# Low halves of weights: computed once, kept in DRAM and read back by later uses

## The chip, the cores and the metric

The kernel runs on one core of a Trainium2 chip. The metric is the device time of one execution in microseconds (us). Three timed runs of the kernel before gave 3698.6, 3701.6 and 3713.3 us, median 3701.6.

## What is computed

One inference step of a one-layer decoder trunk on 1024 prompt tokens and 8 sample tokens, all in float32. Cut to what matters here:

```
h  = rms_norm(x);  p = h @ w_in            # 7168 columns: q, k, v, conv inputs u, memory q, 3 gate blocks
a  = dilated attention(q, k, v);  m = attention into 256 memory tokens;  b = causal conv of the GLU of u
merged = gate_A * (a @ w_a_proj) + gate_B * (b @ w_b_proj) + gate_M * (m @ w_m_proj)
x1 = x + merged @ w_o
h2 = rms_norm(x1);  q = h2 @ w_pq          # 8 heads x 2 halves: product-key scores, top 16, experts and gates
y  = x1 + sum over chosen experts of gate * gelu(h2 . u_e) * v_e       # 16384 experts
```

## The kernel before, in words

**Split products.** A float32 matrix product is made of three matmuls (`mm3`, L173): each operand is split into a high half (a cast to a shorter format, in float32r) and a low half (what is left), and high x high, high x low and low x high are summed in PSUM. For weights this is done by `load_w` (L161). It takes one tile of 128x1024 float32 (512 KB) and three pools of buffers, two each: `wraw` for the loaded tile, `whi` for the high half, `wlo` for the low half. A DMA on SyncE's queue (SP) fills `wraw`, ScalarE (ACT) casts it into `whi` (L158), VectorE (DVE) subtracts the high half from it into `wlo` (L159). The names in the profile are `wr_`, `wh_` and `wl_` and the name of the weight.

**Stages.** `mem_stage` prepares the memory keys and values (8 weight tiles). `front(0)` does the first 512 prompt tokens and the 8 samples: projections k, v, q0, q1, q2, qm (24 weight tiles), conv inputs u (8), 24 gate tiles (`gate`, L652) and 12 tiles of the three branch projections (`gate_proj`, L671), with the attention between them. `tail("0")` does w_o (8 tiles) and, in `topk`, the 16 tiles of w_pq for these tokens. `front(1)` does the same 68 tiles for the second 512 prompt tokens. Then come two tails of 256 tokens each, `1a` and `1b`, again with 8 tiles of w_o (`o1a`, `o1b`) and 16 of w_pq (`pq1a`, `pq1b`) each. So the weights of the first half are loaded and split a second time for `front(1)`, and those of the tail a second and a third time. In tail 1a half of the w_pq tiles use a second set of buffers (`wx`, with one raw buffer). `peer_dense` (L1064) then runs through the 16384 experts densely for the first 640 tokens, while `peer_gather` (L957) fetches the chosen expert rows of the other 384 tokens and of the samples by indirect DMAs that GpSimd (POOL) issues, and DVE does their sums. `gate_build` (L1017) makes the dense gate matrix in DRAM (`gscr`, 2 MB a store) during `front(1)` and tail 1b.

**What sets the order.** The program is recorded with priorities, and a scheduler places each instruction by a model of the times. What results is a fixed order on each engine and on each engine's DMA queue. A DMA that waits for its buffer holds up every later DMA of its queue. TensorE (PE) takes its matmuls in the fixed order too.

## Time and profile before

| | |
|---|---|
| profiled execution, its own time | 3706.1 us |
| its span, first to last instruction | 3704.2 us |
| median of the three timed runs | 3701.6 us |
| TensorE matmul busy | 3434.1 us, 93% |
| TensorE weight load busy | 3014.3 us, 81% |
| VectorE busy | 2901.0 us, 78% |
| ScalarE busy | 1497.1 us, 40% |
| GpSimd busy | 577.5 us, 16% |
| DMA traffic | 902 MB, mean 244 GB/s |

The busy share of an engine over the whole span mixes stages. The stages can be told apart by the times at which ACT casts the tiles of each weight: `front(0)` and its tail take up to some 840 us, `front(1)` 840 to 1557 us, tail 1a 1557 to 1668 us, tail 1b 1658 to 1862 us, where the dense stage begins. A busy matmul row counts a matmul from its start to its modelled end, and these overlap; the weight load row does not overlap with itself.

### The profile page before, as it was taken

Reading aid. Unit: us, or ns where it says so; the run is one execution under the profiler, and the core shown is the slowest. Engines: PE = TensorE matmul, PEld = TensorE weight load, DVE = VectorE, ACT = ScalarE, POOL = GpSimd, SP = SyncE. Lnnn points to the kernel's source line nnn. Section 1 sums busy time; section 2 is a strip of 40 time slices with the busy share of each in tenths; the row PEclk is TensorE's granted clock in tenths of the full one; section 3 lists DMA queues with packets and bytes.
Section 4 is the critical chain, followed back from the end, with each engine's and each line's share of the span. In section 5 each row is a group of like instructions: output and inputs, shape, how many; then the busy total and the mean of one; then the engine's idle time right before and its main releaser. Section 6 shows DMA issues by size and latency. Waiting matters only on the chain.

```text
span 3704.2 us, 55195 instructions
## 1 busy us (share of the span) xinstructions
PE 3434.1 (93%) x19969; PEld 3014.3 (81%) x19969; DVE 2901.0 (78%) x6275; ACT 1497.1 (40%) x3517; POOL 577.5 (16%) x398
## 2 busy tenths in 40 slices
PE   8987989898899989887899999999989999999999
PEld 6766979697677778676798988989878889898988
DVE  4358555499998656779988888888878988897978
ACT  6554552235754445344443333333333333232322
POOL 0000000000000000000003333232323232332322
PEclk9997999999999989898799999999999999999999
DMA  5467455423354445763578988899889888888987
GB/s 182 132 207 256 149 199 157 150 90 116 109 185 168 167 168 188 253 214 131 196 237 315 341 318 326 304 351 327 323 296 350 317 333 324 317 331 299 341 301 273
DMA packets 338454, 902.09 MB, mean 244 GB/s; under 512 B 32588, under 2 KB 140276, under 8 KB 285436
## 3 DMA queue, kind: packets, MB, share of 16 engines
q1 hardware_dynamic: 281732, 487.49, 39.1%
q0 software_dynamic: 56448, 411.07, 28.9%
q8 instruction: 157, 2.57, 0.3%
q14 instruction: 117, 0.96, 0.1%
HBM read 804.09 MB, written 94.83 MB: 243 GB/s over the span
## 4 chain that ended last, share of the span: by engine, by line
PE 38%; issue 23%; DVE 15%; DMA 14%; POOL 8%; ACT 3%; SPq 0%; POOLq 0%; DVEq 0%; ACTq 0%
POOL uv L982 8%; DMA uv<-in_uv,idxB 4%; PE pg L175 2%; PE pg L174 2%; DMA vr<-in_v_tab 2%; PE pg L176 2%; PE pa L174 2%; PE pa L176 2%; PE pa L175 2%; PE pv L174 2%; PE pv L175 2%; PE pv L176 2%; PE pG L1058 1%; PE pG L1057 1%; DMA wko<-kscr 1%
## 5 line engine op out<-in xcount | busy, mean ns | idle before, releaser
L982 POOL DMA_INDIRECT uv<-in_uv,idxB x384 | 567.6, 1478 | 1529.0 <-DVE gacc L996 1196.1
L176 PE MATMUL pa<-h2Ah,ul 128*128 128x320 f32 x2048 | 633.9, 310 | 7.0 <-DVE ul L159 6.8
L174 PE MATMUL pa<-h2Ah,uh 128*128 128x320 f32 x2048 | 635.3, 310 | 2.6 <-ACT ge L1103 1.5
L175 PE MATMUL pa<-h2Al,uh 128*128 128x320 f32 x2048 | 634.0, 310 | 0.0
L986 DVE CUSTOM_DVE_ANT_0 uv<-uv,gh 128x1024 f32<-128x1024 f32 x392 | 477.1, 1219 | 122.1 <-DMA uv<-in_uv,idxB 117.8
L174 PE MATMUL pv<-vh,hh 128*128 128x512 f32 x1280 | 479.6, 396 | 41.5 <-ACT vh L158 28.4
L996 DVE SCALAR_TENSOR_TENSOR gacc<-uv,av,gacc 128x1024 f32<-128x1024 f32 x392 | 501.5, 1279 | 15.2 <-ACT av L994 9.5
L175 PE MATMUL pv<-vl,hh 128*128 128x512 f32 x1280 | 504.1, 394 | 5.2 <-DVE vl L159 5.0
L176 PE MATMUL pv<-vh,hl 128*128 128x512 f32 x1280 | 498.5, 393 | 0.0
L176 PEld LDWEIGHTS pa<-h2Ah,ul 128*128 128x128 f32 x2048 | 386.0, 189 | 11.9 <-DVE ul L159 8.6
L174 PEld LDWEIGHTS pa<-h2Ah,uh 128*128 128x128 f32 x2048 | 386.7, 189 | 7.4 <-ACT ge L1103 3.0
L175 PEld LDWEIGHTS pa<-h2Al,uh 128*128 128x128 f32 x2048 | 386.1, 189 | 2.4
L158 ACT CAST vh<-vr 128x512 fp32r<-128x512 f32 x256 | 157.5, 619 | 460.1 <-PE pv L176 239.4
L174 PEld LDWEIGHTS pv<-vh,hh 128*128 128x128 f32 x1280 | 242.5, 190 | 94.5 <-ACT vh L158 31.4
L175 PEld LDWEIGHTS pv<-vl,hh 128*128 128x128 f32 x1280 | 243.0, 190 | 56.8 <-DVE vl L159 8.8
L176 PEld LDWEIGHTS pv<-vh,hl 128*128 128x128 f32 x1280 | 242.8, 190 | 50.4
L982 POOL DMA_INDIRECT uv<-in_uv,idxS x8 | 9.2, 1156 | 1570.3 <-ACT co L740 1529.2
L159 DVE TENSOR_TENSOR vl<-vr,vh 128x512 fp32r<-128x512 f32 x256 | 175.2, 686 | 83.6 <-ACT vh L158 83.2
L174 PE MATMUL pg<-hTh,wh_g 128*128 128x260 f32 (+1 forms) x576 | 195.1, 339 | 4.0 <-ACT tg L660 4.0
L158 ACT CAST uh<-ur 128x1024 fp32r<-128x1024 f32 x128 | 134.2, 1048 | 152.5 <-PE pa L175 116.5
L175 PE MATMUL pg<-hTl,wh_g 128*128 128x260 f32 (+1 forms) x576 | 194.9, 338 | 0.0
L176 PE MATMUL pg<-hTh,wl_g 128*128 128x260 f32 (+1 forms) x576 | 194.4, 337 | 0.0
(558 smaller groups left out, 7524.1 us busy)
## 6 DMA issues: line engine op xcount, KB each, us to landing
ur<-in_uT SPq DMA_DIRECT2D x128, 512.0 KB
vr<-in_v_tab SPq DMA_DIRECT2D x256, 256.0 KB
gscr<-stg SPq DMA_DIRECT2D x20, 2048.0 KB
Gt<-gscr SPq DMA_DIRECT2D x32, 1280.0 KB
wr_g<-in_w_col SPq DMA_DIRECT2D x48, 512.0 KB
wr_q<-in_w_in SPq DMA_DIRECT2D x24, 512.0 KB
wr_u<-in_w_col SPq DMA_DIRECT2D x16, 512.0 KB
wr_pq<-in_w_col SPq DMA_DIRECT2D x16, 512.0 KB
```

Source lines behind the costliest of these rows:

```text
L158: nc.scalar.copy(hi, raw)
L159: nc.vector.tensor_tensor(lo, raw, hi.bitcast(F32), op=OP.subtract)
L174: nc.tensor.matmul(out, ah, bh, start=start, stop=False)
L175: nc.tensor.matmul(out, ah, bl, start=False, stop=False)
L176: nc.tensor.matmul(out, al, bh, start=False, stop=stop)
L982: nc.gpsimd.indirect_dma_start(out=uv, out_offset=None, in_=I["uv"], in_offset=bass.IndirectOffsetOnAxis(ap=col, axis=0),)
L986: nc.vector.tensor_tensor_reduce(out=uv[:, 0:D], in0=uv[:, 0:D], in1=h2, scale=1.0, scalar=0.0, op0=OP.mult, op1=OP.add, accum_out=av[:, s ...
L996: nc.vector.scalar_tensor_tensor(acc, uv[:, D:], av[:, j : j + 1], acc, op0=OP.mult, op1=OP.add)
L1057: nc.tensor.matmul(pG[:, q], o2[:, a, :, q], wh[:, a, :, q], start=True, stop=False)
L1058: nc.tensor.matmul(pG[:, q], o2[:, a, :, q], wl[:, a, :, q], start=False, stop=True)
```

## The change

`load_w` gets a key. At the first use of a key the tile is split as before, and the low half is also stored to a DRAM tile of its own by a DMA that GpSimd issues. At a later use of the same key ACT casts the high half as before, and the low half is loaded from that DRAM tile by a second DMA on SP's queue, in place of the subtraction on DVE. The keys do not hold the number of the half or of the tail, so `front(1)` and the tails 1a and 1b read what `front(0)` and tail 0 stored. The memory stage and the dense stage have no keys.

```diff
+        lows = {}
+
-        def load_w(wp, src, a, b, name, nraw=2):
+        def load_w(wp, src, a, b, name, nraw=2, key=None):
+
             raw = wp.tile([P, 1024], F32, tag="wraw", bufs=nraw, name=f"wr_{name}")
             hi = wp.tile([P, 1024], F32R, tag="whi", bufs=2, name=f"wh_{name}")
             lo = wp.tile([P, 1024], F32R, tag="wlo", bufs=2, name=f"wl_{name}")
             nc.sync.dma_start(raw.rearrange("p (a b) -> p a b", a=a), src)
-            split_load(raw, hi, lo)
+            if key in lows:
+                nc.scalar.copy(hi, raw)
+                nc.sync.dma_start(lo.bitcast(F32), lows[key])
+            else:
+                split_load(raw, hi, lo)
+                if key is not None:
+                    lows[key] = dram.tile([P, 1024], F32, name=f"low_{key}")
+                    nc.gpsimd.dma_start(lows[key], lo.bitcast(F32))
...
-                        wh, wl = load_w(wp, w_in[:, 2 * kk : 2 * kk + 2, w0 : w0 + 512], 2, 512, f"{name}{hf}{kk}")
+                        wh, wl = load_w(wp, w_in[:, 2 * kk : 2 * kk + 2, w0 : w0 + 512], 2, 512, f"{name}{hf}{kk}", key=f"{name}_{kk}")
...
-                    gh, gl = load_w(wp, w_col[8 + gi], KD, P, f"g{hf}{gi}")
+                    gh, gl = load_w(wp, w_col[8 + gi], KD, P, f"g{hf}{gi}", key=f"g_{gi}")
...
-                wh, wl = load_w(wx if own else wp, w_col[32 + hc], KD, P, f"pq{tid}{hc}", 1 if own else 2)
+                wh, wl = load_w(wx if own else wp, w_col[32 + hc], KD, P, f"pq{tid}{hc}", 1 if own else 2, key=f"pq_{hc}")
```

The calls for u, the branch projections and w_o get a key in the same way. Counted over the program, 92 tiles are stored (24 + 8 + 24 + 12 in `front(0)`, 8 + 16 in tail 0) and 116 are loaded back (68 in `front(1)`, 24 in each of the tails 1a and 1b). The scheduler places everything anew, and line numbers move by 10 in the changed kernel.

At two places the order shows what moves. The first is SP's DMA queue in tail 1b, before: `wr_pq1b` are the raw tiles of w_pq, in the order of their numbers, `h2scr` is the store of the normed tokens.

```order
L165 DMA wr_pq1b_18274<-in_w_col 128x1024
L798 DMA x1scr<-x_1b_17967 128x1024
L798 DMA x1scr<-x_1b_17969 128x1024
L165 DMA wr_pq1b_18324<-in_w_col 128x1024
L801 DMA h2scr<-h_1b_18126 128x1024
L801 DMA h2scr<-h_1b_18149 128x1024
L165 DMA wr_pq1b_18374<-in_w_col 128x1024
L165 DMA wr_pq1b_18424<-in_w_col 128x1024
```

The same queue at the same place, in the changed kernel; `wl_pq1b_18460` is the low half of the tile whose raw load is `wr_pq1b_18458`, `low_pq` its copy in DRAM.

```order
L168 DMA wr_pq1b_18508<-in_w_col 128x1024
L808 DMA x1scr<-x_1b_18151 128x1024
L808 DMA x1scr<-x_1b_18153 128x1024
L811 DMA h2scr<-h_1b_18310 128x1024
L811 DMA h2scr<-h_1b_18333 128x1024
L171 DMA wl_pq1b_18460<-low_pq_7825 128x1024
L168 DMA wr_pq1b_18558<-in_w_col 128x1024
L171 DMA wl_pq1b_18510<-low_pq_7926 128x1024
L168 DMA wr_pq1b_18608<-in_w_col 128x1024
```

A low load now stands between the raw loads, ahead of the raw load of the tile two further on (18558 behind 18460), so that this raw load comes after the moment at which the low buffer is free.

The second place is DVE in the projections of `front(1)`, before: `oh`, `rk` and `iv` belong to the top-16 search of tail 0, `raw_q`, `ra_q` and `rb_q` to the rotary step of q.

```order
L214 TENSOR_TENSOR rb_q_0_12398<-raw_q_0_12381,c_rope 128x4x16
L217 TENSOR_TENSOR rb_q_0_12398<-raw_q_0_12381,c_rope 128x4x16
L205 TENSOR_TENSOR raw_q_128_12404<-raw_q_128_12404,c_qn_a 128x512
L908 TENSOR_TENSOR oh_9534<-oh_9534,iv_9453 128x2048
L159 TENSOR_TENSOR wl_q_12539<-wr_q_12537,wh_q_12538 128x1024
L220 TENSOR_TENSOR raw_q_0_12381<-ra_q_0_12397,rb_q_0_12398 128x4x32
```

The same step of q on DVE in the changed kernel.

```order
L224 TENSOR_TENSOR rb_q_0_12582<-raw_q_0_12565,c_rope 128x4x16
L227 TENSOR_TENSOR rb_q_0_12582<-raw_q_0_12565,c_rope 128x4x16
L922 TENSOR_TENSOR oh_9718<-oh_9718 128x128x8
L868 CAST iv_9737<-ix_7818 128x256
L215 TENSOR_TENSOR raw_q_128_12588<-raw_q_128_12588,c_qn_a 128x512
L230 TENSOR_TENSOR raw_q_0_12565<-ra_q_0_12581,rb_q_0_12582 128x4x32
```

The subtraction between the search and the rotary step is gone; of 216 subtractions for weight tiles on DVE 100 are left.

## Rows read from the trace of the kernel before

**Rows 1.** The page's part 1: busy time, share, instructions.

```profile
PE 3434.1 (93%) x19969; PEld 3014.3 (81%) x19969; DVE 2901.0 (78%) x6275; ACT 1497.1 (40%) x3517; POOL 577.5 (16%) x398
```

**Rows 2.** Stretches: length; busy PE, PEld, DVE, ACT, POOL (instructions); clock, DMA share, GB/s.

```profile
204.00:351.00 147.00, 112.11 (x657) 94.52 (x655) 106.01 (x492) 65.56 (x210) 0.00 (x0) 0.84 0.76 254
...
842.00:1016.00 174.00, 150.22 (x655) 118.03 (x655) 171.63 (x721) 114.36 (x298) 0.00 (x0) 0.96 0.35 109
...
1557.00:1600.00 43.00, 31.34 (x110) 22.74 (x109) 33.09 (x42) 13.17 (x22) 5.01 (x4) 0.88 0.75 282
1600.00:1668.00 68.00, 59.13 (x446) 56.78 (x444) 53.32 (x209) 32.22 (x56) 0.00 (x0) 0.92 0.55 188
1668.00:1698.00 30.00, 25.38 (x119) 19.76 (x118) 29.94 (x152) 10.16 (x15) 0.00 (x0) 1.00 0.45 156
1698.00:1795.00 97.00, 76.40 (x559) 71.55 (x560) 96.97 (x331) 49.79 (x81) 4.00 (x2) 0.89 0.40 147
...
1862.00:3704.00 1842.00, 1784.60 (x9889) 1617.51 (x9887) 1567.07 (x2110) 598.29 (x1343) 561.48 (x380) 0.99 0.86 316
```

**Rows 3.** Waits of PE in 200:420, 800:1000, 1200:1400, 1700:1870: us in total, times, longest.

```profile
PE pS_w L319 <- DVE wao L321: 19.8, 14, 6.1
...
PE p_q L175 <- DVE wl_q L159: 10.3, 4, 6.1
...
PE wT L380 <- DMA wkp<-kscr: 10.2, 3, 7.6
PE wT L380 <- DMA wko<-kscr: 7.2, 3, 3.0
...
PE tr_t1b L190 <- DVE h_1b L183: 11.2, 1, 11.2
```

**Rows 4.** Groups of instructions: busy us, mean ns of one, then idle before them.

```profile
L159 DVE TENSOR_TENSOR wl_g<-wr_g,wh_g 128x1024 fp32r<-128x1024 f32 x48 | 58.7, 1222 | 58.5 <-ACT wh_g L158 58.3
...
L174 PEld LDWEIGHTS pq1b<-h2h1b,wh_pq1b 128*128 128x128 f32 x128 | 25.9, 204 | 7.5 <-ACT wh_pq1b L158 6.4 <-ACT h2h1b L170 1.1
```

**Rows 5.** Stretches, of line L159 (subtractions) alone: length, DVE busy, clock, DMA.

```profile
842.00:1016.00 174.00, 28.84 (x24) 0.96 0.35 109
1016.00:1557.00 541.00, 53.71 (x44) 0.93 0.53 185
1557.00:1862.00 305.00, 62.17 (x51) 0.87 0.53 191
```

**Rows 6.** Timeline of ACT by tile: casts, ns min/median/max, first and last start.

```profile
L158 ACT CAST wh_k<-wr_k x4: 1047/1047/1051, 841.9 to 870.4; 128x1024 fp32r<-128x1024 f32 x4
...
L158 ACT CAST wh_u<-wr_u x8: 1031/1047/1059, 1016.4 to 1091.7; 128x1024 fp32r<-128x1024 f32 x8
...
L158 ACT CAST wh_pq1b<-wr_pq1b x16: 1038/1047/1062, 1697.9 to 1790.2; 128x1024 fp32r<-128x1024 f32 x16
```

**Rows 7.** Timeline of PE in the dense stage, 512-column matmuls: start, us.

```profile
3698.17 0.39 PE L175 MATMUL pv<-vl,hh 128*128 128x512 f32 x1
...
3699.76 0.39 PE L176 MATMUL pv<-vh,hl 128*128 128x512 f32 x1
```

**Rows 8.** Timeline of SP's queue, DMA issues: start, us of the issue.

```profile
1647.42 0.38 SPq L165 DMA_DIRECT2D wr_o1b<-in_w_o  x1
```

**Rows 9.** The chain of work that ended last, 1215:1345 and 1580:1870: start, us.

```profile
1233.36 11.45 DMA wko<-kscr
...
1302.08 15.60 DMA wko<-kscr
...
1610.76 5.14 DMA h2scr<-h_1a
1615.98 3.98 DMA wr_pq1a<-in_w_col
...
1662.90 4.48 DMA wr_pq1a<-in_w_col
...
1739.91 3.28 DMA wr_pq1b<-in_w_col
```

More of the change, by code (lines that the diff above doesn't have):

```diff
@@ L564, in front @@
                     glu = mx.tile([P, 30 + NT], F32, tag="glu", bufs=2, name=f"glu{hf}{cb}")
-                    u1h, u1l = load_w(wp, w_col[cb], KD, P, f"u1{hf}{cb}")
-                    u2h, u2l = load_w(wp, w_col[4 + cb], KD, P, f"u2{hf}{cb}")
+                    u1h, u1l = load_w(wp, w_col[cb], KD, P, f"u1{hf}{cb}", key=f"u1_{cb}")
+                    u2h, u2l = load_w(wp, w_col[4 + cb], KD, P, f"u2{hf}{cb}", key=f"u2_{cb}")
                     for c0, cn in chunks:
@@ L672, in gate_proj @@
                     for fp in range(4):
-                        ph, pl = load_w(wp, w_pr[br][:, :, fp * 256 : fp * 256 + 256], 4, 256, f"p{br}{hf}{fp}")
+                        ph, pl = load_w(wp, w_pr[br][:, :, fp * 256 : fp * 256 + 256], 4, 256, f"p{br}{hf}{fp}", key=f"p{br}_{fp}")
                         for f in (2 * fp, 2 * fp + 1):
@@ L779, in tail @@
                         for kk in range(4):
-                            wh, wl = load_w(wp, w_o[:, 2 * kk : 2 * kk + 2, gs], 2, 512, f"o{tid}{cg}{kk}")
+                            wh, wl = load_w(wp, w_o[:, 2 * kk : 2 * kk + 2, gs], 2, 512, f"o{tid}{cg}{kk}", key=f"o{cg}_{kk}")
                             for j in range(2):
```

## The prediction, made before the changed kernel ran

> **What bounds the kernel now.** I read the page's busy times first: PE 93%, DVE 78% [rows 1]. That average hides where DVE is the limit, so I cut the span into stages and read busy time by stretch [rows 2]. The dense stage, 1862 to 3704 us, is half of the time: PE 1784.6 of 1842 us, DVE 1567.1. It has no keyed weights, so nothing of the change reaches it but its start; I keep its length. In two stretches ahead of it DVE is full. **Stretch A** is the projections of `front(1)`, 842 to 1016 us: DVE 171.6 of 174 us, while the weight loads of PE fill only 118.0. **Stretch B** is the tails: DVE 29.9 of 30 us in 1668 to 1698 and 97.0 of 97 us in 1698 to 1795, with PE's weight loads at 19.8 and 71.6. The waits of PE say the same: 10.3 us for low halves of q, 11.2 us for the normed rows of 1b, both from DVE [rows 3]. In 1600 to 1668 us (the w_pq tiles of 1a) PE's weight loads take 56.8 of 68 us and DVE 53.3: there PE is the limit, and DVE's relief is worth little.
>
> **What is removed.** 116 subtractions, one 1.22 us [rows 4]. In stretch A they are 24, 28.8 us; in the rest of `front(1)` 44, 53.7 us; in the tails 51 subtractions stand in 1557 to 1862 us with 62.2 us [rows 5], of which some 47 are keyed, 57 us. Only what lies where DVE is the limit is gained.
>
> *Stretch A.* 24 tiles go from 841.9 to 1016.4 us, 7.27 us a tile [rows 6]. DVE without the subtractions needs 171.6 - 28.8 = 142.8 us: 31 us less than the stretch. PE needs 24 matmuls of 512 columns a tile; in an unhindered row they start 1.59 / 7 = 0.227 us apart [rows 7], so 5.45 us a tile, 131 us: 43 us less. So DVE stays the nearer limit, with at most 31 us to gain. An engine at 98.6% owes that to a backlog that can always be worked on; once its reserve is gone it will wait for PE now and then. I take 0.7 of it: **-22 us**, bounds -31 and 0.
>
> *Stretch B.* In 1698 to 1795 us stand the 16 subtractions of 1b, 16 x 1.22 = 19.5 us; 0.7 of it is 14 us. The 16 tiles of w_o and the wait of 11.2 us for the normed rows [rows 3] hang on DVE in part; I take 8 us for them together. **-22 us**, bounds -45 (all 57 us less what 1a cannot use, since PE is full there) and 0.
>
> **What is added to the second half.** 116 loads of 512 KB on SP's queue. The new chain for tile i: its low buffer is free when PE has finished tile i-2; then SP issues the load (0.38 us an issue [rows 8], 0.4 here), it lands L later, and PE may go on. Before, ACT and DVE filled that place in 1.05 + 1.22 us [rows 4, 6]. With two buffers a tile cannot take less than (L + 0.4 + p) / 2, p being PE's own time for a tile. The order on SP shows the low load ahead of the raw load of tile i+2, so it does not queue behind that one. L has no row, as no such load exists. The nearest are raw loads of the same size for which the chain waited: 3.28, 3.98 and 4.48 us [rows 9]; at the other end stand attention loads of half the size that came behind other transfers, 11.45 and 15.60 us [rows 9]. I take **L = 4.7 us**, near the first, because in A the DMA engines are busy at 0.35 and in 1b at 0.40 [rows 2], and add a little for the doubled traffic. The limits are then:
>
> - A, p = 5.45: (4.7 + 0.4 + 5.45) / 2 = 5.3 us, below the 5.95 us that DVE's 142.8 us allow.
> - pq1b, p = 24 x 0.204 = 4.9 [rows 4]: 5.0 us, against (1790.2 - 1697.9) / 15 = 6.15 us a tile now [rows 6].
> - o1a and o1b, p = 12 x 0.227 = 2.7: 3.9 us, against some 5.3 now (8 tiles in the 43 us of 1557 to 1600 us).
> - pq1a has two sets of buffers, four low halves in flight, and is not held by L.
>
> The Trainium skill, page "DMA: Bandwidth & Descriptors", section "Anatomy of one DMA", fits a DMA issued from GpSimd as 2.0 us plus its bytes at 436 GB/s, which for 512 KB makes an estimate of 3.2 us. The shortest of the three rows, 3.28 us, agrees and the other two are up to 1.3 us longer; with 3.2 us the w_o tiles would take 3.15 us, 16 x 0.75 = 12 us less, and the sum would be 3662 instead of 3674.
>
> In `front(1)` behind A a tile comes every (1557 - 1016) / 44 = 12.3 us, between attention work, so an L of up to some 11.8 us is hidden. Yet a low load that waits for PE holds up the attention loads behind it in the queue, and PE waits for such loads already, 10.2 + 7.2 us in 1200 to 1400 us [rows 3]. Against that DVE loses 53.7 us of work it has time for. I take **+6 us**, bounds -10 and +20. The traffic: B carries 305 x 191 GB/s = 58 MB [rows 5], plus 47 x 0.524 = 25 MB; in 283 us that is 293 GB/s. The dense stage shows 316 GB/s held for 1842 us [rows 2], so it fits, without much room.
>
> **What is added to the first half.** 92 stores of 512 KB from GpSimd's queue, which is empty there. A low buffer may be rewritten only when its store has landed. The tile two further on needs it: the low half of i is ready about when PE starts i-1 and its buffer's next content is needed at PE's start of i+2, three tiles of 30 x 0.227 = 6.8 us (30 matmuls with the samples' block), less 3.5 us for split and issue, so some 17 us of cover. The nearest row, a 512 KB store to DRAM, took 5.14 us [rows 9]. So the hold costs nothing; were the cover gone, each us beyond 17 would cost a us a tile. What remains is traffic: 48 MB. Only in 204 to 351 us are the DMA engines busy at 0.76 (254 GB/s) [rows 2], and PE waits there for attention on DVE, 19.8 us [rows 3], which waits for loads. The 8 stores of u fall into it, 4.2 MB, 16 us at that rate. I take **+6 us**, bounds 0 and +16.
>
> **Sum.** -22 - 22 + 6 + 6 = -32 us: 3706.1 - 32 = 3674 us against the profiled execution's own time. The median of the runs lies 4.5 us below that execution, so I forecast **3670 us**.
>
> **Rivals.**
>
> *The lows come late: slower.* Same chain, L = 9 us, as low loads queue behind 2 MB stores of `gscr`, `h2scr` stores and each other; the attention loads at 11 to 16 us [rows 9] speak for it, DMA shares of 0.35 to 0.45 against it. Then A takes 7.4 us a tile (+3 us), pq1b 7.1 (+15), w_o 6.05 (+12), with the +6 and +6 of above: +42, or 3744 as a median. It decides from L of about 7.5 us: there A gains 14 us, pq1b loses 4, w_o nothing, and with the +12 the sum is about zero.
>
> *Relief without gain.* DVE is freed, but PE then waits for low loads or for ACT about as long as it did for DVE (L of 6.5 to 8), or the scheduler's new order gives the gain back in the dense stage, where 57 us of idle PE time stand [rows 2] and shift with every order. For it: PE is 93% busy [rows 1]. Time 3690 to 3715, middle 3702.
>
> *More than forecast.* DVE's limit falls fully in A (-31) and B (-40), and the added waits stay at +6: -65, 3637 us.
>
> That the subtractions stay is no rival: the order has 100 of 216 left.
>
> **How the numbers follow.** Forecast (3650 to 3690) 0.45, relief without gain 0.24, late lows (3720 to 3790) 0.22, more than forecast 0.09. The range 3637 to 3745 leaves out about half of each outer case, 0.15. The forecast's own range is 3650 to 3690. Half a per cent, about what a measurement of this kernel can tell, is 18.5 us: faster below 3683, slower above 3720. Of the forecast 0.05 lies above 3683. So faster 0.40 + 0.09 = 0.49, same 0.24 + 0.05 = 0.29, slower 0.22.
>
> **What would show it.** A right: the 24 tiles of the projections in some 152 us instead of 174.5, with no PE wait for `wl_q`. B right: the 16 casts of pq1b in some 78 us instead of 92, the dense stage starting some 30 us earlier and lasting as long as before. L right: PE waits for `wl_` loads of a few us in all in the tails. Late lows would show as PE waits on DMA `wl_pq1b` and `wl_o1b` of over 30 us; a wrong first half as a later start of tail 0; a wrong dense stage as a length other than 1842 us by over 10 us.

## The result and the profile after

The changed kernel takes 3743.6 us in the median against 3700.9 us for the kernel before in the same comparison: ratio 1.0096, 95% interval 1.0073 to 1.0119 (the two medians alone give 1.0115). The time lies within the range given, but on the wrong side: it is slower, where faster was the likeliest. The profiled execution has a span of 3746.6 us, 42.4 more than before.

The page's part 1 of the changed kernel, to be held against [rows 1]: DVE has lost 116 instructions and 124 us, PE's work is the same, and the time went up all the same.

```profile
PE 3429.9 (92%) x19969; PEld 3016.1 (81%) x19969; DVE 2777.1 (74%) x6159; ACT 1499.8 (40%) x3516; POOL 616.0 (16%) x490
```

To find where, the times at which ACT casts the first tile of each weight are taken from both traces as marks [rows 6]. Here are three of them in the timeline of ACT of the changed kernel.

```profile
L170 ACT CAST wh_k<-wr_k x4: 1046/1048/1054, 870.7 to 901.2; 128x1024 fp32r<-128x1024 f32 x4
...
L170 ACT CAST wh_u<-wr_u x8: 1040/1051/1060, 1028.5 to 1100.5; 128x1024 fp32r<-128x1024 f32 x8
...
L170 ACT CAST wh_pq1b<-wr_pq1b x16: 1046/1050/1060, 1731.5 to 1820.1; 128x1024 fp32r<-128x1024 f32 x16
```

`front(1)` begins at 870.7 us instead of 841.9: **the first half lost 29 us**. The projections of `front(1)` (stretch A) take 157.8 us instead of 174.5: 17 gained. From there to o1a 546.7 instead of 540.7: 6 lost. From o1a to the last cast of pq1b 244.9 instead of 233.1: 12 lost. From there to the end 1926.5 instead of 1914.0: 12 lost. Together +42.

The stretches of the changed kernel, with the columns of [rows 2]: the branch projections of `front(0)` and w_o of tail 0, then stretch A, the w_pq tiles of 1b, and the dense stage.

```profile
579.00:674.00 95.00, 81.78 (x681) 76.00 (x681) 45.83 (x92) 20.81 (x29) 6.40 (x12) 0.98 0.66 205
674.00:740.00 66.00, 57.59 (x267) 43.27 (x267) 20.86 (x31) 11.05 (x13) 4.26 (x8) 0.95 0.58 185
...
870.00:1028.00 158.00, 147.31 (x664) 117.87 (x663) 152.19 (x727) 116.60 (x305) 0.00 (x0) 0.98 0.64 210
1731.00:1830.00 99.00, 82.90 (x615) 77.53 (x614) 87.26 (x320) 51.36 (x86) 4.57 (x4) 0.91 0.74 271
1890.00:3746.00 1856.00, 1786.79 (x9883) 1620.09 (x9881) 1558.99 (x2049) 595.41 (x1339) 550.80 (x380) 0.98 0.86 313
```

The first two lines are the loss of the first half: the same 12 and 8 tiles took 75.7 and 58.2 us before. PE now fills 81.78 of 95.00 us of the first; in the kernel before it filled nearly all of it:

```profile
577.00:653.00 76.00, 74.77 (x618) 73.64 (x617) 47.98 (x95) 21.06 (x30) 0.00 (x0) 1.00 0.54 165
653.00:711.00 58.00, 54.62 (x254) 40.53 (x254) 19.50 (x28) 10.16 (x12) 0.00 (x0) 1.00 0.40 132
```

Not all that the first stretch grew by is waiting. Between its marks it grew by 19.6 us: PE is idle for 12.0 us more, and busy for 7.6 us more. Its instructions rose from 618 to 681 because the new order places 72 of the 192 matmuls of the samples' attention (`spaw`) in it; before, all of them stood ahead of it.

What DVE waited for there, in the changed kernel from 579 to 740 us (us in total, times, longest):

```profile
DVE th L694 <- DMA th<-gtscr: 20.4, 8, 4.5
DVE merged L694 <- DMA th<-gtscr: 15.0, 6, 4.5
```

The same two waits in the kernel before, from 577 to 711 us:

```profile
DVE th L684 <- DMA th<-gtscr: 11.3, 8, 2.8
...
DVE merged L684 <- DMA th<-gtscr: 1.6, 1, 1.6
```

`th` are the gate tiles, 130 KB each, which each step of a branch projection reloads from `gtscr`; they have three buffers. 35 us of waits stand where 13 stood, and PE waits for DVE in its turn (`py` is its output for the branch projections, `po` for w_o). In the changed kernel, 579 to 674 us and then 674 to 740 us:

```profile
PE py L184 <- DVE th L694: 9.9, 7, 2.8
PE py L184 <- DVE merged L694: 3.1, 3, 1.6
...
PE po L184 <- DVE th L694: 6.7, 1, 6.7
```

In the kernel before, 577 to 653 us and then 653 to 711 us:

```profile
PE py L174 <- DVE th L684: 1.1, 4, 0.5
...
PE po L174 <- DVE th L684: 2.4, 1, 2.4
```

The landing of each reload can be counted from the traces, from the start of its issue on SP to its last landing record. Over the 48 reloads the median is 2.7 us in the kernel before (longest 4.0) and 4.3 us in the changed kernel (longest 6.6).

PE's waits for low halves in the second half, in 870 to 1028, 1575 to 1632, 1698 to 1731 and 1731 to 1830 us. They are there, some 22 us in all:

```profile
PE p_q L185 <- DMA wl_q<-low_q: 4.6, 3, 2.1
...
PE po1a L185 <- DMA wl_o1a<-low_o: 6.7, 4, 3.6
...
PE po1b L185 <- DMA wl_o1b<-low_o: 3.7, 4, 1.6
...
PE pq1b L186 <- DMA wl_pq1b<-low_pq: 6.6, 5, 3.5
```

How long a low load takes stands in the chain that ended last, tails of the changed kernel (start, us):

```profile
1645.96 5.02 DMA wl_pq1a<-low_pq
...
1709.69 4.57 DMA wl_o1b<-low_o
...
1754.43 6.41 DMA wl_pq1b<-low_pq
1763.82 4.59 DMA wl_pq1b<-low_pq
1782.24 7.20 DMA wl_pq1b<-low_pq
...
1803.52 11.93 DMA wl_pq1b<-low_pq
```

### The profile page after: what moved, and what is told of

Read it like the earlier page. It is cut to its first block, busy times and chain, and to the rows that moved or that the text cites. A ratio compares the mean times of both kernels' runs of the same rounds, so it can differ in the third digit from the quotient of the medians.

```text
span 3746.6 us, 55402 instructions
## 1 busy us (share of the span) xinstructions
PE 3429.9 (92%) x19969; PEld 3016.1 (81%) x19969; DVE 2777.1 (74%) x6159; ACT 1499.8 (40%) x3516; POOL 616.0 (16%) x490
## 4 chain that ended last, share of the span: by engine, by line
PE 22%; issue 20%; DMA 8%; POOL 6%; DVE 2%; ACT 1%; POOLq 0%; SPq 0%; DVEq 0%; ACTq 0%
POOL uv L992 6%; PE pa L184 3%; PE pa L185 3%; PE pa L186 3%; DMA uv<-in_uv,idxB 3%; PE pv L184 3%; PE pv L186 3%; PE pv L185 3%; DMA vr<-in_v_tab 2%; DMA wl_pq1b<-low_pq 1%; DMA uv<-in_uv,idxS 1%; DMA ur<-in_uT 1%; DVE gacc L1006 0%; DMA wl_o1b<-low_o 0%; PE pq1a L184 0%
## 5 line engine op out<-in xcount | busy, mean ns | idle before, releaser
L992 POOL DMA_INDIRECT uv<-in_uv,idxB x384 | 555.4, 1446 | 1534.8 <-DVE gacc L1006 1222.2
L184 PEld LDWEIGHTS pa<-h2Ah,uh 128*128 128x128 f32 x2048 | 386.6, 189 | 16.5 <-ACT ge L1113 9.3
L159 DVE TENSOR_TENSOR vl<-vr,vh 128x512 fp32r<-128x512 f32 x256 | 175.8, 689 | 96.0 <-ACT vh L158 95.7
L159 DVE TENSOR_TENSOR ul<-ur,uh 128x1024 fp32r<-128x1024 f32 x128 | 156.6, 1223 | 52.0 <-ACT uh L158 51.7
```

What stands on the lines that cost most here:

```text
L159: nc.vector.tensor_tensor(lo, raw, hi.bitcast(F32), op=OP.subtract)
L184: nc.tensor.matmul(out, ah, bh, start=start, stop=False)
L992: nc.gpsimd.indirect_dma_start(out=uv, out_offset=None, in_=I["uv"], in_offset=bass.IndirectOffsetOnAxis(ap=col, axis=0),)
```

## The experiments

All runs by the same marks, from one profiled execution each, in us: p is the length of the branch projections of `front(0)` (first cast of p to first cast of o), then the start of `front(1)`, stretch A, `front(1)` from its start to o1a, from o1a to the last cast of pq1b, and from there to the end. The ratio is that of the timed runs to those of the kernel before in the same comparison. A profiled execution need not be a typical one: that of `th4` was the slowest of ten, 18 us above their median, and that of `stores_only` the fastest of four, 20 us below it.

| kernel | p | front(1) starts | A | front(1) | tails | to the end | ratio (95%) |
|---|---|---|---|---|---|---|---|
| before | 75.7 | 841.9 | 174.5 | 715.2 | 233.1 | 1914.0 | 1 |
| before_again | 76.9 | 840.2 | 174.6 | 713.2 | 235.7 | 1900.5 | |
| after | 95.3 | 870.7 | 157.8 | 704.5 | 244.9 | 1926.5 | 1.0096 (1.0073-1.0119) |
| after_again | 97.8 | 869.2 | 157.1 | 702.7 | 244.4 | 1927.1 | |
| stores_only | 96.4 | 867.2 | 163.3 | 719.0 | 225.5 | 1926.5 | 1.0167 (1.0125-1.0208) |
| stores_quarter | 79.9 | 843.6 | 176.6 | 720.5 | 225.9 | 1957.6 | 1.0134 (1.0086-1.0181) |
| stores_tiny | 76.3 | 835.2 | 173.7 | 699.6 | 225.4 | 1934.3 | 1.0006 (0.9987-1.0025) |
| stores_halves | 89.7 | 854.4 | 155.3 | 685.5 | 241.8 | 1927.4 | 1.0059 (1.0038-1.0081) |
| loads_only | 77.0 | 842.3 | 162.7 | 692.8 | 235.2 | 1917.3 | 0.9991 (0.9963-1.0019) |
| no_lows | 76.9 | 838.5 | 161.0 | 682.4 | 214.7 | 1916.7 | 0.9865 (0.9828-0.9902) |
| keys_proj_u | 76.3 | 845.0 | 166.8 | 695.9 | 225.3 | 1939.7 | 1.0034 (1.0015-1.0053) |
| keys_front | 82.3 | 848.2 | 163.0 | 688.7 | 229.8 | 1945.9 | 1.0031 (1.0010-1.0052) |
| keys_no_p | 81.6 | 852.1 | 156.8 | 696.8 | 248.0 | 1897.9 | 0.9994 (0.9977-1.0011) |
| keys_no_po | 82.1 | 846.7 | 157.9 | 695.8 | 250.0 | 1932.6 | 1.0082 (1.0055-1.0109) |
| loads_act | 98.8 | 874.1 | 161.2 | 699.0 | 246.3 | 1907.4 | 1.0063 (1.0044-1.0081) |
| tail1b_lows4 | 95.7 | 866.2 | 157.7 | 707.6 | 241.0 | 1933.3 | 1.0107 (1.0052-1.0162) |
| sub_pool | 75.8 | 838.6 | 188.7 | 734.9 | 224.0 | 1950.7 | 1.0173 (1.0147-1.0200) |
| th4 | 81.7 | 835.6 | 158.1 | 698.7 | 243.9 | 1931.9 | 0.9989 (0.9973-1.0004) |
| before_th4 | 72.4 | 831.3 | 174.5 | 717.0 | 222.7 | 1928.8 | 1.0026 (1.0009-1.0044) |
| th4_lows4 | 80.6 | 839.5 | 158.1 | 701.3 | 236.2 | 1910.3 | 0.9930 (0.9911-0.9949) |

### Stores alone, loads alone, neither

Stores alone (`stores_only`):

```diff
-            if key in lows:
-                nc.scalar.copy(hi, raw)
-                nc.sync.dma_start(lo.bitcast(F32), lows[key])
-            else:
-                split_load(raw, hi, lo)
-                if key is not None:
-                    lows[key] = dram.tile([P, 1024], F32, name=f"low_{key}")
-                    nc.gpsimd.dma_start(lows[key], lo.bitcast(F32))
+            split_load(raw, hi, lo)
+            if key is not None and key not in lows:
+                lows[key] = dram.tile([P, 1024], F32, name=f"low_{key}")
+                nc.gpsimd.dma_start(lows[key], lo.bitcast(F32))
```

> The 92 stores of low halves stay, every later use subtracts again as before, and nothing is read back. Theory 1 (the store traffic of the first half costs it 29 us, the reloads of gate tiles `th` waiting behind it): first cast of `front(1)` at about 871 us instead of 842, and the whole 3730 us against 3701. Theory 2 (the 42 us come from the low loads, which come late in the second half; the later start of `front(1)` is only the scheduler's new order): first cast near 842 us and 3701 us, within 8 us.

`front(1)` started at 867.2 us: theory 1 for the first half. The whole, 3760 us in the median, was 30 us worse than it said. The profiled execution took 3740 us and is 9 us longer behind the first half than the kernel before, where its program is the old one in another order; where the slower executions lose the rest is not shown.

Loads alone (`loads_only`), in place of the store of each tile:

```diff
-                    lows[key] = dram.tile([P, 1024], F32, name=f"low_{key}")
-                    nc.gpsimd.dma_start(lows[key], lo.bitcast(F32))
+                    if not lows:
+                        lows["one"] = dram.tile([P, 1024], F32, name="low_one")
+                        nc.gpsimd.dma_start(lows["one"], lo.bitcast(F32))
+                    lows[key] = lows["one"]
```

> One low half is stored once, and all 116 later uses load that one tile in place of their own, so the 91 other stores are left out and the low halves of the second half belong to another tile (the result is altered, the work is not). Theory 1 (stores cost 29 us, loads net 13): first cast of `front(1)` at 842 us, the whole about 3714 us. Theory 2 (the loads cost it all): 3735 to 3745 us.

`front(1)` at 842.3 us, the whole 3698.8 us, level with before: theory 2 is out, and even the 13 us of theory 1 did not come. That all loads read one tile here did not make them quick: those of pq1b landed in 4.55 us in the median, against 4.66 us in the changed kernel (counted as for `th`).

Neither (`no_lows`):

```diff
             if key in lows:
                 nc.scalar.copy(hi, raw)
-                nc.sync.dma_start(lo.bitcast(F32), lows[key])
+                lo = hi
...
-                    lows[key] = dram.tile([P, 1024], F32, name=f"low_{key}")
-                    nc.gpsimd.dma_start(lows[key], lo.bitcast(F32))
+                    lows[key] = key
```

> No stores, no low loads and no subtraction in the second half: the matmuls take the high half where the low half stood (the result is altered). This is the relief of DVE alone, with nothing that replaces it. Theory 1 (DVE bounds the projections of `front(1)` and the tails, as the prediction had it): the projections take 145 to 155 us instead of 174.5, pq1b some 78 us instead of 92, and the whole is 3640 to 3665 us. Rival (PE and the attention loads take over at once): projections above 160 us and tails as before, 3685 us or more.

3653.3 us, ratio 0.9865: the relief is there, 45 us in this one order. pq1b took 79.0 us, as expected. Stretch A took 161.0 us where 145 to 155 were expected, and no less than the 157.8 with low loads: there the loads cost nothing that shows in the length, although PE waits 4.6 us for them, and near 160 us DVE is no longer full. Stretch A of this kernel (columns of [rows 2]): DVE is idle for 7 of 161 us, where before it was idle for 2 of 174 [rows 2].

```profile
838.00:999.00 161.00, 147.65 (x659) 118.44 (x659) 153.70 (x721) 114.05 (x298) 0.00 (x0) 0.97 0.39 121
```

### What in the stores costs the first half

A quarter of each tile (`stores_quarter`; the diff is against `stores_only`), 16 columns (`stores_tiny`), and two halves (`stores_halves`, low loads kept):

```diff
-                lows[key] = dram.tile([P, 1024], F32, name=f"low_{key}")
-                nc.gpsimd.dma_start(lows[key], lo.bitcast(F32))
+                lows[key] = dram.tile([P, 256], F32, name=f"low_{key}")
+                nc.gpsimd.dma_start(lows[key], lo.bitcast(F32)[:, 0:256])
```

> As the kernel with the stores alone, but each of the 92 stores writes a quarter of its tile, 128x256, 128 KB. If the bytes cost the time, a quarter of 29 us: first cast of `front(1)` at about 849 us and 3708 us as a whole. If the number of stores or the scheduler's new order costs it: 871 us and 3730 us, as with whole stores.

> The 92 stores write 128x16 elements each, 8 KB, and nothing is read back. If the bytes cost the first half its 25 us (the reloads of `th` behind the stores): first cast of `front(1)` at 842 to 844 us. The dense stage has no stores in it; from its first cast of `uh` to the end it took 1864 us before, 1864 with whole stores, 1901 with quarter stores. If that spread is the scheduler's new order, it will lie anywhere in 1864 to 1901 here too, and the whole at 3700 to 3745 us; if it is traffic, 1864 us and 3700 us.

> The changed kernel with each store made as two of 128x512, 256 KB: the same bytes and the same low loads, but the scheduler orders the program anew. First cast of `front(1)`: 866 to 873 us if the bytes cost the first half its time, over 880 us if it is the number of stores. What lies behind it has no stores: from the first cast of o1a to the end 2171 us passed in the changed kernel, and 2146, 2154 and 2153 us in three other orders with low loads. If this part of the loss belongs to the one order, it comes out at 2145 to 2160 us here and the whole at 3720 to 3735 us; if it belongs to the change, 2165 us or more and 3740 us or more.

As many stores with fewer bytes: `front(1)` at 843.6 and 835.2 us, so the bytes cost the 25 to 29 us, not the number. The reloads of `th` say the same: their median landing is 2.9 us with the tiny stores, 3.2 with the quarter, 4.1 with whole stores and with halves. The stretch of the branch projections with quarter stores is nearly that of before, PE 75.62 of 80.00:

```profile
573.00:653.00 80.00, 75.62 (x612) 74.40 (x611) 46.12 (x92) 20.68 (x28) 6.47 (x12) 0.98 0.55 170
```

Two things went against the expectations. The quarter stores cost 50 us as a whole, nearly all from the last cast of pq1b to the end (1957.6 us against 1914.0), where no store is left. And the same bytes in halves cost the first half only 12 us. The marks tell how: p is 14 us longer than before and the stretch behind it 7, but p begins at 568.5 us instead of 577.3, so the bytes cost 21 us there too. Why p begins earlier in this order was not looked into.

Without the stores of the 12 branch projection tiles (`keys_no_p`):

```diff
+            if key is not None and not (not key.startswith('p') or key.startswith('pq')):
+                key = None
```

> All keys but those of the 12 tiles of the branch projections. If the stores among the reloads of `th` cost the first half its time: branch projections of `front(0)` 76 to 80 us instead of 95, w_o of tail 0 still some 64 us instead of 58, `front(1)` from about 850 us. If the scheduler's earlier gates or the traffic elsewhere cost it: about 865 us. The whole, with the second half as in the changed kernel: about 3725 us by the first, 3740 us by the second.

p 81.6 us and `front(1)` at 852.1 us, near what the first reading said. PE is busy for 80.0 of the 81.6 us, with the 72 `spaw` matmuls among them, and the reloads land in 2.9 us in the median, so no waiting is left there. The whole came out at 3696 us, level with before and 48 below the changed kernel, since the last stretch was the shortest of all.

A fourth buffer for the gate tiles (`th4`), the bytes as in the changed kernel. One of five places is shown; `tu`, `sq`, `ts` and `tg`, earlier tiles in the same ring of buffers, get the same edit:

```diff
-                                th = mx.tile([P, 512], F32, tag="gt", bufs=3, name=f"th{br}{hf}{f}{c0}")
+                                th = mx.tile([P, 512], F32, tag="gt", bufs=4, name=f"th{br}{hf}{f}{c0}")
```

> The changed kernel with four buffers in place of three for the gate tiles `tg` and `th` (tag gt). The order from the tails on is nearly that of the changed kernel. If the stores cost the branch projections their time by making each reload of `th` land later, with three of them in flight, a fourth takes that back: branch projections of `front(0)` 76 to 82 us instead of 95, first cast of `front(1)` at 850 to 858 us instead of 871, the whole 3725 to 3732 us instead of 3744. If the stores hold the DMA engines or another queue in a way that buffers don't help, 92 us or more and no change in the whole.

More than expected: `front(1)` starts at 835.6 us, and the whole, 3694.3 us, is 49 us below the changed kernel. The branch projections of this kernel, 566 to 647 us (columns of [rows 2]), and PE's wait there:

```profile
566.00:647.00 81.00, 78.34 (x679) 73.78 (x679) 47.76 (x95) 20.59 (x30) 6.38 (x12) 1.00 0.79 244
```

```profile
PE py L184 <- DVE th L694: 1.7, 3, 1.1
```

The DMA engines are busier than in the changed kernel, 0.79 against 0.66, and PE no longer waits. So it was not the rate of the transfers but the landing time of each reload, with three of them in flight: 48 reloads in 75.7 us are 1.58 us each, a turn of three buffers in 4.7 us; in the changed kernel 95.3 / 48 x 3 = 6.0 us. The reloads land no sooner here, in 4.2 us in the median. In a turn of 4.7 us that leaves half a us for the DVE instructions that free the buffer, 0.42 us each and two of them in two of the three branches, and half of the reloads take longer still; a turn of four, 4 x 1.58 = 6.3 us, has room for them.

Only part of the 35 us can be put to this. `front(1)` starts 35.1 us earlier than in the changed kernel: 13.6 us come in p and 7.8 behind it, but 13.7 ahead of it, before any reload, as p begins at 565.8 us instead of 579.5. Those may come from the same ring, which serves the gates there, or from the order, since `stores_halves` with three buffers begins p at 568.5 us as well; no run separates the two.

The same in the kernel before (`before_th4`, the same edit):

> The kernel before with four buffers of tag gt in place of three, nothing else. If the fourth buffer only repairs what the stores did: branch projections of `front(0)` 74 to 76 us as before, `front(1)` from 838 to 842 us, the whole within 12 us of 3700 us. If the ring of three held the kernel before as well: `front(1)` from 825 to 835 us and the whole 3680 to 3690 us, and of the 49 us that it gave the changed kernel only some 35 are owed to the stores.

`front(1)` starts at 831.3 us, 10 earlier, so some 10 of the 35 us that the fourth buffer gave the changed kernel come without any stores. As a whole it gained nothing: 1.0026, the last stretch took 15 us more.

### The low loads of the second half

From ACT's queue (`loads_act`):

```diff
-                nc.sync.dma_start(lo.bitcast(F32), lows[key])
+                nc.scalar.dma_start(lo.bitcast(F32), lows[key])
```

> The changed kernel with the low loads issued by ACT on its own queue instead of SP's; stores as they are, so `front(1)` from about 870 us again. If low loads that wait for their buffer hold up the raw loads and attention loads behind them on SP's queue, the second half gets shorter: from the first cast of `front(1)` to the last of pq1b 925 to 940 us instead of 949. If the loads are late because the DMA engines are full, or ACT's own casts now wait behind the issues, it stays within 10 us of 949 or gets longer.

From the start of `front(1)` to the last of pq1b 945.3 us against 949.4: within 10 us, so a queue that is held up on SP is not what counts, unless ACT's casts, which now wait behind the issues, took back what it gave.

Two more low buffers in tail 1b (`tail1b_lows4`):

```diff
+            wq = left.enter_context(tc.tile_pool(name="wq1b", bufs=1)) if tid == "1b" else None
...
-            lo = wp.tile([P, 1024], F32R, tag="wlo", bufs=2, name=f"wl_{name}")
+            lo = (wq or wp).tile([P, 1024], F32R, tag="wlo", bufs=2, name=f"wl_{name}")
...
-                wh, wl = load_w(wx if own else wp, w_col[32 + hc], KD, P, f"pq{tid}{hc}", 1 if own else 2, key=f"pq_{hc}")
+                wh, wl = load_w(wx if own else wp, w_col[32 + hc], KD, P, f"pq{tid}{hc}", 1 if own else 2, key=f"pq_{hc}", wq=wq if hc % 2 else None)
```

> The changed kernel with two more low buffers for the w_pq tiles of tail 1b: every second low half goes to a pool of its own, so a low load waits for the matmuls of the tile four back instead of two back. The order on the engines is nearly that of the changed kernel, so this is a direct comparison. If two buffers and the landing time make the low loads late (the prediction's chain), the 6.6 us of PE waits for `wl_pq1b` fall to 2 us or less and the 16 casts of pq1b take 82 to 84 us instead of 88.6; the whole gains no more than 6 us, 3738 us. If the loads are late because the DMA engines are busy, the waits stay.

Near what was expected for the two-buffer chain. PE's wait for low halves of pq1b, and the casts of pq1b in the timeline of ACT of this kernel:

```profile
PE pq1b L186 <- DMA wl_pq1b<-low_pq: 2.5, 1, 2.5
```

```profile
L170 ACT CAST wh_pq1b<-wr_pq1b x16: 1037/1050/1066, 1733.3 to 1814.8; 128x1024 fp32r<-128x1024 f32 x16
```

81.5 us instead of 88.6, or of 85.7 in the second execution of the changed kernel; with the fourth `th` the same two buffers make 80.5 us of 90.1 (`th4_lows4` against `th4`). But the 7 us did not reach the end: the last stretch became 7 us longer, 1933.3.

### Fewer keys, another engine, and both rings

Keys for the projections and u (`keys_proj_u`), these and the gates (`keys_front`), these and w_pq (`keys_no_po`), each by a condition as in `keys_no_p`:

> Keys for the 24 projection tiles and the 8 tiles of u alone; gates, branch projections, w_o and w_pq are split at every use as before. Theory (what is stored from 42 to 287 us costs nothing, what is loaded back in 842 to 1140 us saves): first cast of `front(1)` at 842 to 845 us, projections about 158 us instead of 174.5, u some 10 us less, the last cast of pq1b some 25 us earlier than 1790 us, the whole 3675 us if the dense stage keeps 1864 us, up to 3710 us if its order costs what it cost with quarter stores. Rival (each store costs wherever it is): `front(1)` starts 10 us later and the whole is 3690 us or more with a dense stage of 1864 us.

> Keys for the projections, u and the gates alone, so low halves are loaded in `front(1)` only and the tails split as before. `front(1)` from 843 to 845 us; some 698 us to o1a if low loads save there what they saved in four kernels so far (697 to 705 us against 700 to 720 us without); the tails and the dense stage then 2147 to 2183 us, as in five orders without low loads in the tails. Sum 3688 to 3726 us, middle 3705. A kernel faster than before by over 0.5% would need the short end of both.

> Keys for the projections, u, the gates and w_pq; the branch projections and w_o are split at every use. By the stages so far: branch projections of `front(0)` 76 us, w_o of tail 0 58 us, `front(1)` from 844 to 847 us, some 698 us from there to o1a, and 2146 to 2171 us from there to the end: 3690 to 3715 us. With the low loads of w_o gone, PE does not wait for `wl_o1a` (16 us in the kernel without keys for the branch projections alone). Rival: the w_o stores cost nothing and its loads nothing net, so the time is that of that kernel, 3696 us, with `front(1)` from 852 us.

In the stages the first two came near what was expected: `front(1)` from 845 and 848 us, then 696 and 689 us to o1a, the last cast of pq1b 24 us earlier than before in both. But A took 166.8 us in the first, where some 158 were expected. The last stretch then took 1940 and 1946 us, and both kernels are 0.3% slower than before. The third lost in the tails (250.0 us) and in the last stretch: 1.0082, outside what was expected.

GpSimd subtracts in `front(1)` (`sub_pool`; no stores, no loads):

```diff
-            if key in lows:
+            if key in lows and not key.startswith(("pq", "o")):
                 nc.scalar.copy(hi, raw)
-                nc.sync.dma_start(lo.bitcast(F32), lows[key])
+                nc.gpsimd.tensor_tensor(lo, raw, hi.bitcast(F32), op=OP.subtract)
...
-                    lows[key] = dram.tile([P, 1024], F32, name=f"low_{key}")
-                    nc.gpsimd.dma_start(lows[key], lo.bitcast(F32))
+                    lows[key] = key
```

> No stores and no loads: in `front(1)` GpSimd, which is idle there, subtracts in place of DVE; the tails split on DVE as before. If DVE's relief is what counts and a subtraction on GpSimd takes no more than some 3 us and does not slow DVE: front(1) from its first cast to o1a in 685 to 700 us instead of 715, as with low loads, with no cost in the first half: `front(1)` from 842 us, the whole 3680 to 3710 us. If GpSimd is slower than some 6 us a tile, or DVE is slowed beside it, projections of `front(1)` take 175 us or more and the whole 3710 us or more.

The slowest, 1.0173, level with `stores_only`. GpSimd needs 2.4 to 3.8 us a tile, by the means of its groups, which A's 7 us would bear, but DVE is slowed beside it. DVE's instructions in stretch A of this kernel (busy us, mean ns), two of them with two tensor operands, and one that searches one tensor:

```profile
L906 DVE TENSOR_TENSOR rk<-rk,rt 8x128 f32<-8x128 f32 x2 | 4.8, 2402 | 0.0
...
L222 DVE TENSOR_TENSOR ra_k<-raw_k,c_rope 128x128 f32<-128x128 f32 x4 | 4.7, 1178 | 0.0
...
L883 DVE FIND_INDEX8 pu<-sc,cand 128x8 uint32<-128x112 f32 x32 | 8.0, 263 | 0.0
```

and the same in the kernel before:

```profile
L897 DVE TENSOR_TENSOR rk<-rk,rt 8x128 f32<-8x128 f32 x2 | 0.5, 272 | 0.0
...
L213 DVE TENSOR_TENSOR ra_k<-raw_k,c_rope 128x128 f32<-128x128 f32 x4 | 1.1, 265 | 0.0
...
L874 DVE FIND_INDEX8 pu<-sc,cand 128x8 uint32<-128x112 f32 x32 | 7.9, 256 | 0.0
```

DVE is busy for 187.87 of 189 us in A, more than with its own subtractions (columns of [rows 2]).

```profile
838.00:1027.00 189.00, 156.09 (x665) 121.41 (x663) 187.87 (x722) 114.14 (x303) 79.26 (x24) 0.94 0.33 104
```

Both rings (`th4_lows4`, the edits of `th4` and of `tail1b_lows4` in the changed kernel):

> The changed kernel with four buffers of tag gt and with two more low buffers for the w_pq tiles of tail 1b. By the two single runs: `front(1)` from 836 us, pq1b in 82 to 84 us instead of 90, the whole 3685 to 3695 us, that is level with the kernel before or up to 0.4% faster. If tail 1b's gain is given back in the dense stage again, as it was without the fourth `th`, 3690 to 3710 us.

3677.4 us, ratio 0.9930 (0.9911 to 0.9949): faster than both kernels. pq1b took 80.5 us, `front(1)` started at 839.5 us.

### The same orders again

> The kernel before, unchanged, for a second trace of the same order. If the differences behind the tails come from the order, the time from the first cast of o1a to the end is 2147 us again, within 5 us; if they come from execution to execution, it differs by up to 15 us.

> The changed kernel, unchanged, for a second trace of the same order. First half: first cast of `front(1)` at 868 to 873 us again. From the first cast of o1a to the end 2171 us again, within 5 us, if the order sets it; up to 15 us off if it differs from execution to execution.

Up to the tails each repeats within 5 us. The last stretch repeats within 1 us in the changed kernel, and differs by 13.5 us in the kernel before, so a difference of that size in it can come without any change.

## Why the prediction was wrong, step by step

**The first half: +6 forecast, +29 measured. This is the step that turned the sign.** It judged the stores by the busy share of the DMA engines and looked for stretches where that is high. 577 to 711 us, at shares of 0.54 and 0.40, was not looked at. But PE filled 74.77 of 76.00 us there, and behind it stood a ring of three `th` buffers that were just quick enough. What hurt this ring is how late each reload landed, not how full the engines were. Shown: bytes (tiny and quarter stores: `front(1)` from 835.2 and 843.6 us), the place (without p's stores 10 us remain), the landing (in the median 2.7 to 3.0 us in the eleven traces where p's low halves are not stored or only 8 KB of each, 4.1 to 4.6 us in the eight where they are stored whole), and the ring (with a fourth buffer PE's wait for `th` in p falls from 13.0 to 1.7 us while the landing stays at 4.2). Of the 29 us, p's 12.0 us of added idle time and PE's longer wait for the last `th` behind it, 6.7 us instead of 2.4, are this wait; 7.6 us are more PE work in p, some 5 of them `spaw` moved there by the order (PE is busy for 5.5 us more in `keys_no_p`, which has them too), and the remaining 5 were not traced. That the low buffers' hold costs nothing was right: in `front(0)` no split waits for a store.

**Stretch A: -22 forecast, -17 measured.** The reading was right in the main, and DVE has slack there now, 152.19 of 158 us against 171.63 of 174 [rows 2]. PE still waits 4.6 us for `wl_q`, where 10.3 us stood [rows 3]; the forecast was none. The term was over-sized by the share of 0.7; 17 of 31 us are 0.54. How long A takes also hangs on how much of tail 0's search the order leaves in it: `stores_only`, with all 24 subtractions, took 163.3 us, and DVE is full there.

```profile
867.20:1030.50 163.30, 147.01 (x658) 115.44 (x657) 161.00 (x718) 110.25 (x294) 0.00 (x0) 0.99 0.40 124
```

**The rest of `front(1)`: +6 forecast, +6 measured**, by luck in part: four kernels that split everything in `front(1)` with DVE took 700 to 721 us for the whole of it, mean 714 (`stores_only`, `stores_quarter`, `stores_tiny`, `before_th4`), eleven with low loads for some or all of its tiles 685 to 708, mean 697. So low loads are worth some 17 us in `front(1)`; the relief without them some 32 (682.4, one order).

**Stretch B: -22 forecast, +12 measured up to the last cast of pq1b.** Three parts failed. The first is the cost of a load: L was taken as 4.7 us at the DMA shares of the kernel before, and as the same for every tile. The median was right (4.66 us over the 16 loads of pq1b, issue to landing), but the loads themselves raise pq1b's share from 0.40 [rows 2] to 0.74; single loads take 6.41, 7.20 and 11.93 us, the mean is 5.56, and the raw loads beside them land in 5.14 us instead of 3.18 in the median, which the forecast did not count. With four buffers pq1b takes 81.5 us, so it was the two-buffer chain, and PE's waits for low halves in the tails are 17 us, not a few. One side sum was wrong as well: 3662 instead of 3674 us takes 12 us off because w_o tiles would need 3.15 instead of 3.9 us, but the 3.9 us, below the 5.3 of before, had cost the 3674 nothing.

The second is the relief itself. That DVE was full in pq1b was read right, but the 92 us were one order's: seven kernels that split all of tail 1b on DVE, in other orders, took 80.3 to 86.0 us for pq1b, and `no_lows`, without subtractions, 79.0. DVE is full there too (79.7 of 80.3 us in `before_th4`); less of its other work falls between the tiles. The casts of `stores_tiny`, against [rows 6]:

```profile
L158 ACT CAST wh_pq1b<-wr_pq1b x16: 1045/1049/1057, 1679.9 to 1760.2; 128x1024 fp32r<-128x1024 f32 x16
```

So a new order alone gave most of the 14 us that the forecast put to the relief, and with the low loads and two buffers pq1b took 83 to 98 us.

The third is that what the tails lose or gain does not stand as such at the end. From o1a to the end, eight kernels without low loads in the tails took 2147 to 2184 us, mean 2164, and nine with them 2146 to 2183, mean 2164: on the mean the low loads gain nothing there. Without either it was 2131, in one execution of one order, 5 us below the second execution of the kernel before (2136), so what the relief alone is worth there is not shown.

**The dense stage: kept in length, +12 measured.** The stage has no keys, and two kernels that differ only in the size of their stores in the first half took 1934 (tiny) and 1958 us (quarter) for the last stretch. The scheduler's new order is the likely source; it differs on every engine even between kernels that have the same instructions there. It is not the only one: `stores_only` and `keys_proj_u` have the same order of PE's matmuls from the first dense one on, and differ by 13 us, as do two executions of the kernel before (1914.0 and 1900.5). Against these the changed kernel loses 12 and 26 us. Which work in it makes the difference was not found. PE's waits for `dacc`, the dense stage's running sum, do not tell: 12.9 us before, 26.4 after and 42.5 with quarter stores, but 16.5 in the second execution of the changed kernel, whose last stretch is as long.

**The rival that gave the number**, late lows with 3744 us, was right only by accident: it wanted over 30 us of PE waits for `wl_o1b` and `wl_pq1b`; 10.3 stand there. The true sum is 29 in the first half, 11 gained in `front(1)`, and 24 behind it, in which the low loads and the order were not separated. That the +43 is no fixed price of the change is shown by `th4` and `th4_lows4`: the same stores and loads, with two rings deepened, are level with the kernel before and 0.7% faster.

Whether stores from another queue than GpSimd's would have hurt `th` less was not tried.

## What to carry to other kernels

Added traffic is to be costed at the shallowest ring of buffers that it passes, by the time in which a turn of that ring must come round, and not by the busy share of the DMA engines alone; where PE is full and a shallow ring feeds it, hold the landing time of one reload against a turn of the ring. One more buffer there is the first thing to try with any edit that adds DMAs. And where a scheduler orders the program anew, a control that changes the order and next to no work (here the tiny stores at +0.1% and the quarter stores, with a quarter of the bytes, at +1.3%) tells how much of a difference of 1% can belong to the order. It also shows whether a full engine is full in every order: here pq1b took 92 us in one and 80 us in others, with the same subtractions.

## What the runs showed of the hardware

A GpSimd subtraction that runs beside DVE lengthens DVE's instructions with two tensor operands, from 272 to 2402 ns for one of 8x128 and from 265 to 1178 ns for one of 128x128, and leaves those that search one tensor alone, 256 and 263 ns. The Trainium skill, page "SBUF — State Buffer", section "SBUF: two separate sides", says that DVE and GpSimd share one pair of ports by an exclusive lock, which a DVE instruction with two inputs from SBUF needs against a GpSimd one that reads it; these rows agree.

A reload of 130 KB, counted from its issue to its last landing record, took 2.7 to 3.0 us in the median of 48 where the branch projections' low halves were not stored or only 8 KB of each, 3.2 us with 128 KB of each stored, and 4.1 to 4.6 us with all 512 KB, whole or in halves, with the DMA engines at 0.54 (before), 0.55 (quarter stores) and 0.66 to 0.79 (the changed kernel and `th4`).

A 512 KB load of a low half took 4.3 to 5.0 us in most rows of the chain and 6.4 to 11.9 us in three, with the DMA engines at 0.74 to 0.89 in the stretches between 1645 and 1830 us; raw loads of that size took 3.28 to 4.48 us at 0.40 to 0.55 [rows 9].
